# HGRN q, HGRN gate and the second value columns of w_in by seven half-size products

## The chip, the cores and the metric

The kernel runs on one core of one Trainium2 chip. The metric is device time in microseconds (us), lower is better; the kernel before was timed in three runs, median 2907.5 us (2903.78 to 2909.04). Besides these, one execution was profiled.

## The reference

One layer of a bidirectional encoder with two parallel groups of heads, for 1024 tokens of 2048 channels, in float32:

```python
u = rmsnorm(h, g_pre)
z = u @ w_in                                   # (1024, 2048) x (2048, 9216)
aq, ak, av, ag, hq, hf_f, hf_b, hv, hg = jnp.split(z, SPLIT_IDX, axis=-1)   # 1024 columns each
...                                            # dilated attention from aq, ak, av -> o_att
y_att = o_att * jax.nn.silu(ag)
qh = jax.nn.silu(heads(hq, HG_HEADS))          # 8 heads of 128
vh = heads(hv, HG_HEADS)
o_fw = hgrn2_direction(qh, vh, heads(hf_f, HG_HEADS), lb_f)
o_bw = jnp.flip(hgrn2_direction(jnp.flip(qh, 1), jnp.flip(vh, 1),
                                jnp.flip(heads(hf_b, HG_HEADS), 1), lb_b), 1)
y_hg = rmsnorm(o_fw + o_bw, g_hg).reshape(B, S, HG_W) * jax.nn.silu(hg)
h = h + rmsnorm(jnp.concatenate([y_att, y_hg], axis=-1) @ w_out, g_post)
h = h + rmsnorm(jax.nn.sigmoid(h @ w_pg) * (p @ w_pp), g_ple)
```

`hgrn2_direction` is a gated linear recurrence over the tokens, with f = lb + (1 - lb) * sigmoid(f_logit) as forget gate and 1 - f as key.

## The kernel before

**Products in three parts.** Each float32 matrix product is done as three products: a high part of the activations times the high part and times the low part of the weights, and a low bfloat16 part of the activations times a bfloat16 copy of the weights. The normalised activations u lie transposed in SBUF for the whole projection: `uh` (high, two tiles of 128 channels x 16 channel blocks x 512 tokens, one for each half of the tokens) and `ul` (low, the same shape). A *piece* of weights is 128x512 elements: `raw` is loaded on SP's queue, ScalarE copies it to `wh` (L82), GpSimd subtracts to get the low part `wl` (L83), VectorE casts it to `wb` (L84). Each of `raw`, `wh`, `wl`, `wb` has three buffers. GpSimd and ScalarE and VectorE are called POOL, ACT and DVE in the profile.

**Order of the stages.** First the eight token tiles are normalised and transposed (`prenorm`), with the first value group (columns 2048 to 2559) worked off in between, for tiles 0 and 1, for 2 and 3, and for 4 to 7 (its second half, four token tiles: 12 products of 512 columns for each piece). Then come three value groups `v_group(1)` to `v_group(3)` over all eight token tiles (24 products for each piece, 16 pieces); 2 and 3 are the value columns of the HGRN heads (7168 to 8191). They go through DRAM (`vD`). Then the eight HGRN heads, then the eight pairs of attention heads, then the output product and the gated embedding.

**A head of HGRN.** `hgrn` projects 128 columns at a time with `group` (16 blocks of channels in four pieces, 24 products each, into two PSUM banks of 512 tokens): the forward gate f0, the backward gate f1, q, and late in the head the output gate. `sink_f` takes f0 and f1 out of PSUM (sigmoid on ACT L240, scaling on DVE L241, into `F2`), `gate_evac` takes out q and the gate (x * sigmoid(x), L225 and L226). From f0 and f1 come X and O (L259 to L261, DVE) and their sum KD (L264, POOL); POOL also multiplies neighbouring gates for the next levels (`TB`, L334). The first small products use KD and q (`pl`). Seven levels of the recurrence follow, each some DVE operations (L281) and 32 small products on TensorE (L275, L300, L307). Then transposes (L351), the chunk states (L366 on TensorE, L370 and L372 on DVE), the output products `pout` (L385 to L389), the norm (L391, L392, `rstd2`) and `hon` (L398); `finish` transposes, multiplies by the gate and stores, and is issued after the f0 group of the next head.

**What sets the order.** The kernel is written stage by stage, but the framework's scheduler places the instructions on the engines; `piece` raises the priority of weights outside the value groups. Each engine, and each DMA queue, then works through its own list in order. `gb()` gives four PSUM banks to projections (two groups ahead), `wk()` four to everything else. The buffer `hq` is also that of the transposed keys `hk0` (tag "hq"), and `gt` has one buffer.

## Time and profile before

| | us |
|---|---|
| median of three runs | 2907.5 |
| profiled execution | 2911.69 |
| its span, from the first to the last instruction | 2909.9 |
| first value group with the norm, to | 142 |
| value groups 1, 2, 3, to | 228, 314, 401 |
| HGRN heads, about | 401 to 1314 |
| attention, about | 1314 to 2051 |
| output product and embedding | 2051 to 2910 |

| engine | busy us | share |
|---|---|---|
| TensorE | 2785.7 | 96% |
| VectorE (DVE) | 1508.4 | 52% |
| ScalarE (ACT) | 925.5 | 32% |
| GpSimd (POOL) | 1023.8 | 35% |

The profile is one execution. Matmuls are pipelined, so that the duration of one (about 390 ns) is longer than the time from one to the next, and a TensorE that waits a little between products still looks busy. A row of the view in order of time has start, duration, engine, line, operation, output<-inputs, shape and count, and in brackets the idle time ahead of it and what ended it. A row of a view by stretches has the busy time of each engine in the stretch, then the granted clock of TensorE, the share of the DMA engines and GB/s.

### The profile page before, as it was taken

The numbers are of one execution on the slowest core, as the hardware profiler recorded it, in microseconds if no ns is written. First come the engines' busy times: TensorE is split into PE (matmuls) and PEld (weight loads), VectorE is DVE, ScalarE is ACT, GpSimd is POOL, SyncE is SP. The second block draws the span as 40 slices with busy tenths as digits, with TensorE's granted clock in tenths as the row PEclk, the third lists the DMA queues.
The fourth block names the chain that finished last, engine by engine and source line by source line (L and its number), as shares of the span: only waits on it lengthen the run. The fifth ranks groups of instructions, "written<-read, shape, count | busy, mean of one in ns | idle before, by whom it ended". The sixth has DMA issues, their size and how long they took to land. (4 is left out here: it accounts for less than half of the span.)

```text
span 2909.9 us, 46582 instructions
## 1 busy us (share of the span) xinstructions
PE 2785.7 (96%) x18128; PEld 1885.7 (65%) x18384; DVE 1508.4 (52%) x2833; ACT 925.5 (32%) x1672; POOL 1023.8 (35%) x769
## 2 busy tenths in 40 slices
PE   6999999999999999999999999999999899999997
PEld 4666666676667676676666666666566566665664
DVE  8601116856346346356655555555755645555555
ACT  5311112222122112124434444443533223333323
POOL 2422223413313313322222222222244554666555
PEclk9999999999999999999999999999999999999998
DMA  6412221211111111121221222122344543433453
GB/s 226 121 55 80 77 86 39 66 52 39 57 52 44 52 52 45 51 65 55 78 70 45 73 76 71 47 74 71 113 122 133 159 142 97 131 113 109 146 155 106
DMA packets 251614, 250.54 MB, mean 86 GB/s; under 512 B 21633, under 2 KB 175233, under 8 KB 250241
## 3 DMA queue, kind: packets, MB, share of 16 engines
q1 hardware_dynamic: 242224, 238.62, 27.6%
q10 hardware_dynamic: 9168, 8.93, 0.9%
q8 instruction: 144, 2.36, 0.3%
q14 instruction: 78, 0.63, 0.1%
HBM read 205.54 MB, written 29.36 MB: 81 GB/s over the span
## 5 line engine op out<-in xcount | busy, mean ns | idle before, releaser
L83 POOL TENSOR_TENSOR wl<-raw,wh 128x512 fp32r<-128x512 f32 x568 | 764.7, 1350 | 1599.8 <-ACT wh L82 1507.1
L84 DVE CAST wb<-raw 128x512 bf16<-128x512 f32 x584 | 430.5, 740 | 785.2 <-PE gb L106 281.8
L82 ACT CAST wh<-raw 128x512 fp32r<-128x512 f32 x584 | 358.4, 617 | 1241.7 <-PE gb L101 414.7
L101 PE MATMUL gb<-uh,wh 128*128 128x512 f32 x1792 | 744.3, 415 | 0.0
L102 PE MATMUL gb<-uh,wl 128*128 128x512 f32 x1792 | 708.6, 395 | 0.0
L106 PE MATMUL gb<-ul,wb 128*128 128x512 bf16 x1632 | 405.7, 380 | 9.8 <-issue 1.8
L101 PEld LDWEIGHTS gb<-uh,wh 128*128 128x128 f32 x1792 | 337.1, 188 | 82.9 <-issue 1.2
L102 PEld LDWEIGHTS gb<-uh,wl 128*128 128x128 f32 x1792 | 337.1, 188 | 68.9 <-issue 1.0
L106 PEld LDWEIGHTS <-wb 128*128 128x128 bf16 x1792 | 158.4, 98 | 204.6 <-issue 54.3
L810 PE MATMUL gb<-wh,yh 128*128 128x512 f32 x512 | 231.2, 452 | 2.8 <-DVE Y L842 2.8
L810 PE MATMUL gb<-wh,th 128*128 128x512 f32 x480 | 215.8, 450 | 0.0
L811 PE MATMUL gb<-wl,yh 128*128 128x512 f32 x512 | 203.7, 398 | 4.7 <-POOL wl L83 4.7
L811 PE MATMUL gb<-wl,th 128*128 128x512 f32 x480 | 190.6, 397 | 5.4 <-POOL wl L83 5.4
L645 DVE CUSTOM_DVE_ANT_1 asm<-asc,amask 128x512 f32<-128x512 f32 x128 | 88.3, 690 | 119.9 <-PE asc L639 119.7
L814 PE MATMUL gb<-wb,yl 128*128 128x512 bf16 x479 | 133.7, 383 | 1.6
L814 PE MATMUL gb<-wb,tl 128*128 128x512 bf16 x452 | 126.2, 384 | 1.0
L650 ACT ACTIVATE asm<-asm,anm 128x512 f32<-128x512 f32 x128 | 92.5, 722 | 90.3 <-DVE anm L648 90.0
L810 PEld LDWEIGHTS gb<-wh,yh 128*128 128x128 f32 x512 | 97.6, 191 | 33.3 <-DVE Y L842 3.3
L737 PE MATMUL gb<-wh,uh 128*128 128x512 f32 x256 | 116.4, 461 | 1.4 <-ACT wh L82 1.3
L811 PEld LDWEIGHTS gb<-wl,yh 128*128 128x128 f32 x512 | 97.4, 190 | 24.3 <-POOL wl L83 5.9
L738 PE MATMUL gb<-wl,uh 128*128 128x512 f32 x256 | 102.4, 407 | 10.9 <-POOL wl L83 7.9
L634 PE MATMUL asc<-ak,aqt 128*32 128x256 bf16 x1536 | 109.7, 401 | 3.2 <-issue 2.4
(274 smaller groups left out, 3668.4 us busy)
## 6 DMA issues: line engine op xcount, KB each, us to landing
raw<-in_w_in_dram SPq DMA_DIRECT2D x320, 256.0 KB
raw<-in_w_out_dram SPq DMA_DIRECT2D x128, 256.0 KB
raw<-in_w_pg_dram SPq DMA_DIRECT2D x128, 256.0 KB
xt<-in_x_dram SPq DMA_DIRECT2D x8, 1024.0 KB
vD<-vo SPq DMA_DIRECT2D x32, 256.0 KB
raw<-yD SPq DMA_DIRECT2D x32, 256.0 KB
xr<-in_x_dram SPq DMA_DIRECT2D x32, 256.0 KB
ak<-ak SPq DMA_DIRECT2D x96, 64.0 KB
```

The source lines that it names most:

```text
L82: nc.scalar.copy(wh, raw)
L83: (sub or nc.gpsimd).tensor_tensor(wl, raw, f32(wh), op=ALU.subtract)
L84: nc.vector.tensor_copy(wb, raw)
L101: nc.tensor.matmul(pb[hf], wh[:, k], self.uh[hf][:, kt], start=(kt == 0), stop=False)
L102: nc.tensor.matmul(pb[hf], wl[:, k], self.uh[hf][:, kt], start=False, stop=False)
L106: mm = nc.tensor.matmul(pb[hf], wb[:, k], self.ul[hf][:, kt], start=False, stop=(kt == KT - 1))
L634: t = nc.tensor.matmul(sc[32 * r:32 * r + 32, :256], qb[:, sq, 32 * r:32 * r + 32], KS[s][:, h, r::4], start=(s == 0), stop=False, skip_gr ...
L737: nc.tensor.matmul(pb[t], hi, wh, start=(k == 0), stop=False)
L738: nc.tensor.matmul(pb[t], hi, wl, start=False, stop=False)
L810: nc.tensor.matmul(pb[t], a, pc[0], start=first, stop=False)
L811: nc.tensor.matmul(pb[t], a, pc[1], start=False, stop=False)
L814: nc.tensor.matmul(pb[t], lo[:, k, 128 * t:128 * t + 128], pc[2], start=False, stop=last)
```

## The change

q, the output gate and the second value columns (1024 columns of `w_in` each) are no longer computed by eight products of half the size (two halves of the tokens, of the channels and of the columns) but by seven, after Winograd's form of Strassen's scheme. It needs sums of blocks on both sides:

- **On the activations**, four sums S1 to S4 of blocks of u, the same for all three. `s_build` makes them, for each of the eight channel blocks of a half, with twelve additions and subtractions (nine on DVE, three on POOL) and four copies on ACT, and stores them to DRAM in high and low parts (`sD`). In the text it stands behind `v_group(1)`.
- **On the weights**, T1 to T4. `Block.weights` makes them for each piece: T2 loads three blocks and makes two subtractions and keeps the result in `TB`, T3 loads two and makes one, T1 and T4 load one and subtract `TB`, and three products take a block as it is.
- `Block.product` issues one of the seven: eight pieces of 128 channels, 12 products each into four PSUM banks. The products go in turn to two sets of four banks, two of them on top of what stands there. `Block.run` adds up the four blocks of the result with copies on ACT and additions on DVE.
- The value columns go to `vD` as before. q and the gate are multiplied by their sigmoid (ACT and POOL, `z_out`) and go to DRAM as `zD`, in the order of the heads, ahead of all heads; a head of HGRN loads its rows of them (two loads of 0.5 MB on SP's queue) where it had two groups of products.
- The constants of the heads are placed behind the second value group and the sums; the tiles of `prenorm` get a pool of their own, and `vo` a buffer name that is shared.

```diff
         self.group(w_in, base + 2048, sink_f(1))
         q = big.tile([128, S], F32, name="hq", tag="hq", bufs=1)
-        self.group(w_in, base, lambda hf, p: self.gate_evac(q[:, 512 * hf:512 * hf + 512], p))
+        nc.sync.dma_start(q, self.zD["hq"][h])
...
         gt = big.tile([128, S], F32, name="hgt", tag="gt", bufs=1)
-        self.group(w_in, base + 4096, lambda hf, p: self.gate_evac(gt[:, 512 * hf:512 * hf + 512], p))
+        nc.sync.dma_start(gt, self.zD["hg"][h])
...
+    def s_build(pool, kk):
...
+        (a11, l11), (a12, l12), (a21, l21), (a22, l22) = [
+            (f32(K.uh[r][:, kk + 8 * c]), K.ul[r][:, kk + 8 * c]) for r in range(2) for c in range(2)]
+        x0, x1, x2 = x("sx0"), x("sx1"), x("sx2")
+        add(x1, a21, l21, nc.gpsimd)
+        add(x2, a22, l22, nc.gpsimd)
+        add(x0, a11, l11)
+        add(x2, x1, x2)
+        s2 = x("sx3")
+        sub(s2, x2, x0)
+        sub(x1, x0, x1)
+        sub(x0, a12, s2)
+        add(x0, x0, l12)
+        for i, t in enumerate((x2, s2, x1, x0)):
+            h = pool.tile([128, 512], F32R, name="sxh", tag="sxh", bufs=3)
+            l = pool.tile([128, 512], BF16, name="sxl", tag="sxl", bufs=3)
+            nc.scalar.copy(h, t)
+            sub(l, t, f32(h), nc.gpsimd if i == 3 else V)
+            nc.sync.dma_start(sD[i][0][:, kk], f32(h))
+            nc.sync.dma_start(sD[i][1][:, kk], l)
...
+        def raw(self, kk, r, c, second=False):
+            if second:
+                t = ring_pool[0].tile([128, 512], F32, name="rb", tag="rb", bufs=4)
+            else:
+                t = K.wp.tile([128, 512], F32, name="raw", tag="raw", bufs=3)
...
+            elif name == "T2":
+                t = self.raw(kk, 0, 1)
+                sub(t, t, self.raw(kk, 0, 0, True))
+                d = self.TB[:, kk]
+                sub(d, self.raw(kk, 1, 1, True), t)
+                t = d
+            elif name == "T1":
+                t = self.raw(kk, 1, 1)
+                sub(t, t, self.TB[:, kk])
+            elif name == "T3":
+                t = self.raw(kk, 1, 1)
+                sub(t, t, self.raw(kk, 0, 1, True))
+            else:
+                t = self.raw(kk, 1, 0)
+                sub(t, t, self.TB[:, kk])
...
+            nc.scalar.copy(wh, t)
+            sub(wl, t, f32(wh), nc.gpsimd)
+            V.tensor_copy(wb, t)
...
+                for c in banks:
+                    mm(c, hi, wh, first and kk == 0, False)
+                    mm(c, hi, wl, False, False)
+                for c in banks:
+                    mm(c, lo, wb, False, kk == 7)
...
+        def run(self):
...
+                        nc.sync.dma_start(f32(h), sD[i][0][:, 4 * q:4 * q + 4])
+                        nc.sync.dma_start(l, sD[i][1][:, 4 * q:4 * q + 4])
...
+            self.product(0, orig(0, 0), "11", True)
+            c1 = self.copies(0, "tA")
...
+            self.product(1, orig(0, 1), "21", True)
+            for c in range(4):
+                add(c1[c], c1[c], self.pb[1][c])
+                self.out(0, 0, c, c1[c])
...
+            self.product(0, comb(1), "T2", False)
+            u = self.copies(0, "tB")
...
+            self.product(1, comb(0), "T1", True)
+            p5 = self.copies(1, "tA")
+            self.product(0, comb(2), "T3", False)
...
+            self.product(1, comb(3), "22", False)
...
+            self.product(0, orig(1, 1), "T4", False)
...
+    def z_out(name, pool):
+        def f(r, n, c, t):
+            sg = pool.tile([128, 512], F32, name="zsg", tag="zsg", bufs=2)
+            nc.scalar.activation(sg, t, AF.Sigmoid)
+            nc.gpsimd.tensor_tensor(t, t, sg, op=ALU.mult)
+            nc.sync.dma_start(zD[name][4 * n + c][:, 512 * r:512 * r + 512], t)
...
         v_group(0, (4, 5, 6, 7), p0)
+        v_group(1, tuple(range(8)), p0)
+        with tc.tile_pool(name="p0s", bufs=1) as p0s:
+            for kk in range(8):
+                s_build(p0s, kk)
         with tc.issue_after(late[0].ins), tc.issue_after(late[1].ins):
             K.hg_consts((lb_fwd, lb_bwd), g_hg)
-        for cg in range(1, 4):
-            v_group(cg, tuple(range(8)), p0)
+        with tc.tile_pool(name="p0r", bufs=1) as p0r:
+            ring_pool[0] = p0r
+            Block((7168, 7680), False, v_out(2), p0, False).run()
+            Block((8192, 8704), True, z_out("hg", p0), p0, True).run()
+            Block((4096, 4608), True, z_out("hq", p0), p0, False).run()
```

What stands in the built programs at the places in question (line numbers of each program's own source). First DVE, behind the last normalised tile (L151 writes the low part of u), where the second half of the first value group begins. Before, the casts of its pieces (L84) stand there with the small constants of the heads:

```order
L151 TENSOR_TENSOR ul_97<-xp,uh_95 128x4x128 x10
L84 CAST wb<-raw 128x512
L186 TENSOR_SCALAR hgi<-hgi 128x32
L422 TENSOR_SCALAR ab<-api 128x1
L422 TENSOR_SCALAR arho<-api 128x1
L187 TENSOR_TENSOR hgx<-hgi,hgj 128x32
L422 TENSOR_SCALAR atl<-ab 128x1
```

Now, at the same place (L753 and L756 are the additions and subtractions of `s_build`):

```order
L151 TENSOR_TENSOR ul_97<-xp,uh_95 128x4x128 x10
L84 CAST wb<-raw 128x512
L753 TENSOR_TENSOR sx_1837<-uh_94,ul_96 128x512
L753 TENSOR_TENSOR sx_1839<-sx_1838,sx_1839 128x512
L84 CAST wb<-raw 128x512
L756 TENSOR_TENSOR sx_1844<-sx_1839,sx_1837 128x512
L756 TENSOR_TENSOR sx_1838<-sx_1837,sx_1838 128x512
L756 TENSOR_TENSOR sxl<-sx_1839,sxh 128x512
L756 TENSOR_TENSOR sx_1837<-uh_94,sx_1844 128x512
L84 CAST wb<-raw 128x512
```

The scheduler has moved the sums ahead of the second value group: about four of them stand between two casts of the first one's second half. Of the 72 on DVE, 49 stand ahead of the cast for its last piece. On POOL, before, the subtractions L83 stand alone for the value groups:

```order
L83 TENSOR_TENSOR wl<-raw,wh 128x512 x85
L512 MEMSET apart_4066 128x512
L512 MEMSET apart_4067 128x512
L83 TENSOR_TENSOR wl<-raw,wh 128x512 x6
L334 TENSOR_TENSOR TB<-F_2954 128x1024
```

Now, from the start (19 pieces; POOL has every second piece of the first half of that group, and three of its second half):

```order
L83 TENSOR_TENSOR wl<-raw,wh 128x512 x19
L753 TENSOR_TENSOR sx_1838<-uh_95,ul_97 128x512
L753 TENSOR_TENSOR sx_1874<-uh_95,ul_97 128x512
L753 TENSOR_TENSOR sx_1839<-uh_95,ul_97 128x512
L753 TENSOR_TENSOR sx_1875<-uh_95,ul_97 128x512
L83 TENSOR_TENSOR wl<-raw,wh 128x512 x2
L753 TENSOR_TENSOR sx_1911<-uh_95,ul_97 128x512
L83 TENSOR_TENSOR wl<-raw,wh 128x512
L753 TENSOR_TENSOR sx_1910<-uh_95,ul_97 128x512
```

Of the 24 on POOL, 17 stand ahead of the subtraction for the last piece of that group. Then TensorE in the middle of the heads, where a head's first small products (`pl`, from KD and q) stand. Before, the 96 products of the q group come between the second gate group and these, and the gate group has begun (L101 and L102 are the high products of a group, L106 the low ones):

```order
L106 MATMUL gb<-ul_97,wb 128x512
L101 MATMUL gb<-uh_94,wh 128x512
L102 MATMUL gb<-uh_94,wl 128x512
L101 MATMUL gb<-uh_94,wh 128x512
L275 MATMUL pl<-hq,KD 32x32 x16
L102 MATMUL gb<-uh_94,wl 128x512
L101 MATMUL gb<-uh_94,wh 128x512
L275 MATMUL pl<-hq,KD 32x32 x16
```

Now the second gate group is the last ahead of them, with the 16 high products of the first piece of the next head (whose end is seen here) in between:

```order
L101 MATMUL gb<-uh_95,wh 128x512
L102 MATMUL gb<-uh_95,wl 128x512
L275 MATMUL pl<-hq,KD 32x32 x32
L275 MATMUL pl<-Q_9540,X 32x32 x32
L106 LDWEIGHTS wb
L106 MATMUL gb<-ul_96,wb 128x512
```

Every head from the third on has this order; in the second 56 products stand in that place. Further on, 51 products of the next head stand between the small products of the levels, 10 among the states and the first `pout`, 20 between `pout` and the transposes of `hon`, and 111 from there to the next head's `pl`, 192 in all.

94 lines of the change are left out of this document (88 added, 6 removed).

## The prediction

> **What bounds the kernel now.** First the page's table of engines, for the busiest engine; then the busy times by stage, because a mean over stages with different limits says little.
>
> ```profile
> PE 2785.7 (96%) x18128; PEld 1885.7 (65%) x18384; DVE 1508.4 (52%) x2833; ACT 925.5 (32%) x1672; POOL 1023.8 (35%) x769
> ...
> 98.00:142.00 44.00, 43.90 (x192) 29.10 (x196) 25.04 (x79) 12.40 (x22) 19.31 (x15) 1.00 0.38 92
> 228.00:314.00 86.00, 85.74 (x376) 58.79 (x382) 9.06 (x21) 11.79 (x20) 19.92 (x16) 1.00 0.25 74
> 314.00:401.00 87.00, 86.74 (x381) 59.26 (x387) 10.06 (x22) 12.77 (x22) 20.73 (x17) 1.00 0.24 73
> 401.00:1314.00 913.00, 882.32 (x7790) 634.00 (x7881) 482.28 (x943) 200.09 (x328) 269.37 (x207) 1.00 0.18 54
> ```
>
> The second to fifth rows are the second half of the first value group, the two value groups that the change replaces, and the HGRN heads; columns are PE, PEld, DVE, ACT, POOL busy, granted clock, DMA share, GB/s. TensorE is full in all four, at full clock. So a removed product is worth its issue interval, as long as something else keeps TensorE fed. The interval comes from the casts of a value group, which keep step with the products:
>
> ```profile
> 153.38 0.43 DVE L84 CAST wb<-raw 128x512 bf16<-128x512 f32 x1 [4.86 <-PE vb L741]
> ...
> 223.49 0.43 DVE L84 CAST wb<-raw 128x512 bf16<-128x512 f32 x1 [4.97 <-PE vb L741]
> ```
>
> Thirteen pieces lie between these casts: 5.393 us per piece of 24 products, 0.2247 us per product. What the second value group shows as idle, DVE at a tenth, looks like free room for the sums; the order of the changed program shows that they don't stand there.
>
> **The gain.** q, gate and the two value columns cost 2304 products (768 each); seven eighths is 2016. 288 x 0.2247 = **-64.7 us**. The products stay the same form, so neither the interval nor this term is in doubt; what follows eats into it.
>
> **The sums.** `s_build` adds 72 DVE and 24 POOL operations. In the changed order 49 of the DVE ones and 17 of the POOL ones stand ahead of the weights of the last piece of the first value group's second half, whose last 14 pieces (after two that are ready) still need their `wl` and `wb`. What DVE and POOL do to each other is the question:
>
> ```profile
> 2137.20 0.69 DVE L799 TENSOR_TENSOR yl<-raw,yh 128x512 bf16<-128x512 f32 x1 [1.09 <-ACT yh L798]
> 2137.82 1.53 DVE L84 CAST wb<-raw 128x512 bf16<-128x512 f32 x1
> ...
> 2137.77 1.29 POOL L83 TENSOR_TENSOR wl<-raw,wh 128x512 fp32r<-128x512 f32 x1 [1.94 <-ACT wh L82]
> ...
> 65.17 2.35 DVE L167 SCALAR_TENSOR_TENSOR xt<-xt,xr,gpre 128x2048 f32<-128x2048 f32 x1
> 67.44 1.49 DVE L84 CAST wb<-raw 128x512 bf16<-128x512 f32 x1
> 68.85 1.76 DVE L83 TENSOR_TENSOR wl<-raw,wh 128x512 fp32r<-128x512 f32 x1
> ...
> 65.75 4.32 POOL L83 TENSOR_TENSOR wl<-raw,wh 128x512 fp32r<-128x512 f32 x2 [5.09 <-ACT wh L82]
> ```
>
> The cast of 0.43 takes 1.53 and ends where POOL's operation has ended. Further up two POOL operations of 1.29 take 4.32, since the first can't begin before DVE's of 2.35 is through, and DVE's subtraction of 0.69 takes 1.76 behind the second. So the two engines take turns: casts and two-input operations of DVE never run beside a POOL operation, and their times add. Every operation of `s_build` has two inputs in SBUF. The Trainium skill, "SBUF — State Buffer", section "Who interferes with whom", says the same: a DVE instruction with two SBUF inputs and a GpSimd instruction that reads SBUF exclude each other for a whole instruction. The trace agrees (1.53 against 0.43); without that rule the two engines would overlap, and the build would cost 1 us by the lower bound below.
>
> Start to start, DVE's subtraction takes 0.62 (2137.20 to 2137.82). So 49 x 0.62 + 17 x 1.29 + 14 x (1.29 + 0.43) = 30.4 + 21.9 + 24.1 = 76.4 us of turns.
>
> ```profile
> 94.14 6.14 DVE L151 TENSOR_TENSOR ul<-xp,uh 128x512 bf16<-128x512 f32 x10 [0.57 <-ACT uh L150]
> ...
> 141.90 1.29 DVE L744 COPY vo<-vb 128x512 f32<-128x512 f32 x2 [0.87 <-PE vb L741]
> ```
>
> The sums can't begin before the last activations, at 100.3; the last weights come at 176.7 and their 12 products end at 179.4. Before, they ended at 141.9: **+37 us**. Bounds: if the engines overlapped, POOL alone with 31 x 1.29 = 40.0 ends at 143, +1; if each of DVE's operations waited as in the 1.76 and 1.49 rows, 49 x 1.76 + 14 x 1.49 = 107 us, +68. I take the sum of turns, which is how the rows add up. The rest of the sums (23 and 7) has all of the second value group, 86 us, and is free there. The 64 stores on SP's queue, among the raw loads, move 12.6 MB over more than 80 us, half the rate below.
>
> **The products with two subtractions.** T2 reads three weight blocks per piece where a piece now has 12 products, 2.70 us. The 228 to 314 row moves 74 GB/s at a share of 0.25, so about 296 GB/s at full load (an estimate). T2 loads 24 x 0.262 = 6.3 MB, and beside it go four stores (1.05 MB) and a half of the next sums (1.57 MB): 8.9 MB, 30.1 us, of which 7 blocks (6.2 us) fit the buffers ahead. That is 23.9 us where the last piece is wanted after 18.9: 5 us in each of three blocks, **+15**. Turns of POOL and DVE, 1.29 + 0.43 + 2 x 0.62 = 2.96 per piece, and in the second and third block four multiplications by the sigmoid (5.2) make 23.7 to 28.8 us, of which two ready pieces (5.9) are done before: 18 to 23 against the same 18.9. They lie under the same wait and are not added. Bounds: 0 if the buffers spread it; with nothing ahead 8.5, and T3 (7.3 MB, 24.8 us against 21.6) 3.2 more: 35. The other five products load and split less than 2.70 us per piece; the evacuations fall on the other four banks.
>
> **The heads.** Two of four projections leave each head, 43.1 of
>
> ```profile
> L264 POOL TENSOR_TENSOR KD<-X,O x8: 2392/3280/3282, 449.9 to 1208.8; 128x1024 f32<-128x1024 f32 x8
> ```
>
> (1208.8 - 449.9) / 7 = 108.4 us. That is counted in the gain. But the q group was also cover:
>
> ```profile
> 876.59 1.90 PE L106 MATMUL gb<-ul,wb 128*128 128x512 bf16 x8
> 878.14 0.58 PE L101 MATMUL gb<-uh,wh 128*128 128x512 f32 x1
> ...
> 900.70 0.46 PE L275 MATMUL pl<-hq,KD 128*32 128x32 f32 x32
> ...
> 879.16 0.55 DVE L241 TENSOR_SCALAR F<-F,omlb,lb 128x512 f32<-128x512 f32 x1
> ...
> 880.52 2.13 DVE L260 TENSOR_SCALAR O<-F 128x512 f32<-128x512 f32 x1
> ...
> 901.52 1.23 DVE L262 TENSOR_TENSOR Q<-hq,F 128x1024 f32<-128x1024 f32 x1
> ...
> 879.79 2.58 POOL L334 TENSOR_TENSOR TB<-F 128x1024 f32<-128x1024 f32 x1 [1.22 <-DVE F L241]
> 882.45 1.10 POOL L334 TENSOR_TENSOR TB<-TB 128x512 f32<-128x512 f32 x1
> 883.51 3.28 POOL L264 TENSOR_TENSOR KD<-X,O 128x1024 f32<-128x1024 f32 x1
> ```
>
> The second gate group of a head ends at 878.14. Sigmoid, scaling, two products TB and then KD on POOL end at 886.79, and all 8.65 us lay under the q group; the small products on KD came at 900.70. Now only 16 products of the next head (3.6 us) stand between. TensorE waits 5.05 us in seven heads (in the second head 56 products stand there): 35. At the end of a head:
>
> ```profile
> 942.38 0.39 PE L387 MATMUL pout<-hst,Q 128*128 128x128 f32 x2
> ...
> 946.65 1.29 DVE L398 TENSOR_TENSOR hon<-pout,hr 128x512 f32<-128x512 f32 x2
> ```
>
> the way from the last pout to the normalised tiles takes 5.6 us (to 947.94), under the next head's group; now 20 products, 4.5 us: about 1 us, eight times: 8. Between these ends DVE is the pace,
>
> ```profile
> 907.00:934.00 27.00, 23.64 (x452) 18.06 (x455) 26.40 (x56) 6.47 (x11) 4.75 (x3) 1.00 0.08 22
> ```
>
> (26.4 of 27 us from the second level to the last state), and its operations stay, so fewer products beside them save nothing there: they are what TensorE lacks later. **+43 us.**
>
> What is moved out of the heads costs nothing by itself:
>
> ```profile
> L82 ACT CAST wh<-raw 128x512 fp32r<-128x512 f32 x584 | 358.4, 617 | 1241.7 <-PE gb L101 414.7
> ...
> L225 ACT ACTIVATE sg<-gb 128x512 f32<-128x512 f32 x32 | 19.1, 597 | 10.9 <-PE gb L106 10.9
> ```
>
> the sigmoids (0.6 on ACT) come back in the blocks, where ACT has 0.62 per piece of 2.70 to do. The loads of q and gate (0.5 MB, two per head) go through SP's queue, q behind the wait for the transposed keys that share its buffer, with the raw loads of two later pieces behind it; 125 products (28 us) stand between its issue and its use, and three raw and three split buffers stand between. Without that cover a load from issue to use, as long as a piece, would show in each head.
>
> Bounds of the heads: 8 if KD is covered after all; 72 if DVE's Q product (1.23) pushes KD back and the clock below takes all it can.
>
> A waiting TensorE also slows down:
>
> ```profile
> 68.70 1.12 PE L738 MATMUL gb<-wl,uh 128*128 128x512 f32 x2 [2.13 <-POOL wl L83]
> ...
> 68.00:70.00 2.00, 1.30 (x4) 1.00 (x5) 2.00 (x2) 0.00 (x0) 2.00 (x2) 0.71 0.04 5
> 70.00:72.00 2.00, 2.00 (x8) 1.57 (x8) 2.00 (x5) 0.89 (x2) 0.07 (x1) 0.50 0.50 135
> 72.00:74.00 2.00, 2.00 (x9) 1.36 (x9) 1.71 (x6) 0.32 (x1) 0.00 (x0) 0.94 0.81 247
> ```
>
> After a wait of 2.1 us the granted clock is 0.5 for some 3.5 us, 1.75 us lost. A wait of 5 us in a head will do that; part of it falls on DVE's time: 1 us, seven times, **+7**. The Trainium skill, "TensorE: Matmul & The Clock Gate", part 1, wants an idle window of about 3.4 us for it; by that rule the heads' 5 us would do, by the row shorter waits too, and the sum is the same.
>
> **Sum.** -64.7 + 37 + 15 + 43 + 7 = +37 us. The profiled execution took 2911.7 (span 2909.9 and 1.8 around it), 4 above the median of 2907.5; I put the difference on the median: **2945 us**.
>
> **Rivals.**
> - *Heads stay fed* (not slower): the wait for KD at the head's start decides; its price is 42 of the 50 us. For it: KD's inputs X and O are ready at 882.6, and only the order on POOL puts TB first. Against: 3.6 us of cover for 8.65. Then 2903; above 1 us per head left of the 6, the sign is slower.
> - *Sums overlap*: the engines don't exclude each other for these operations, build +1: 2909. Against it are the rows above. Both together: 2866, faster.
> - *The transfers decide*: T2 and T3 at their upper bound (35) and the heads at 64: 2986. For it: 250 GB/s on average over a block (37.8 MB in 151 us) against 296; against it: the ring loads have long rows.
> - That the count isn't seven eighths is excluded: each block issues 7 x 96 products.
>
> **Chances.** Forecast 0.61; transfers 0.15; heads fed 0.10; sums overlap 0.07; both 0.07. A measurement tells about 0.2% (6 us) from no change. Faster: both, 0.04 of heads fed, 0.02 of overlap, 0.13. Same: 0.05 and 0.04, 0.09. Slower: the rest, 0.78. The range 2897 to 2992 leaves out both together, and the ends of the others.
>
> **What would show it.** The second half of the first value group should end near 179 us, TensorE waiting there for POOL's wl; the second group takes 86 us. Blocks should take 151.0 us of products each and some 5 more, waiting in T2. Heads should repeat every 71 to 72 us with one wait of 5 us ahead of the KD products, and a clock of 0.5 behind it. If the value group ends before 150, or heads repeat in 66, I am wrong.

## The result, and the profile after

The changed kernel takes 2980.5 us (median of four runs, 2974.4 to 2991.5) against 2906.1 (2903.8 to 2909.0): **slower by the factor 1.026**, 95% interval 1.0224 to 1.0295. The profiled execution took 2974.35 with a span of 2972.6, 62.7 more than the span before.

First the engines from the page of the changed kernel, then its busy times by stage (columns as in the table of before: PE, PEld, DVE, ACT, POOL, granted clock, DMA share, GB/s):

```profile
PE 2757.8 (93%) x17841; PEld 1847.2 (62%) x18096; DVE 1800.0 (61%) x3099; ACT 1001.2 (34%) x1810; POOL 1232.3 (41%) x897
...
98.00:142.00 44.00, 33.69 (x129) 20.48 (x130) 44.00 (x44) 13.07 (x23) 32.05 (x22) 0.92 0.55 159
142.00:180.00 38.00, 24.56 (x77) 14.96 (x79) 36.03 (x49) 11.65 (x22) 24.59 (x17) 0.82 0.53 171
180.00:262.00 82.00, 81.74 (x360) 56.22 (x365) 25.66 (x77) 16.14 (x28) 25.18 (x19) 1.00 0.51 176
262.00:746.00 484.00, 467.09 (x1981) 306.56 (x2018) 278.30 (x332) 143.07 (x241) 268.75 (x197) 0.99 0.67 225
746.00:1396.00 650.00, 563.44 (x6336) 412.33 (x6402) 459.88 (x856) 143.45 (x240) 214.68 (x151) 0.96 0.21 63
```

TensorE lost only 28 us of busy time where 64.7 us of products went, and it now stands idle in three stages: the end of the first value group and the start of the second (first two rows, DVE full or nearly, clock down to 0.82), the blocks (262 to 746) and the heads (746 to 1396). Only the third row, the rest of the second value group, is as full as before.

By stage, from the start of one stage's first product to that of the next:

| stage | before | after | without waits | lost |
|---|---|---|---|---|
| to the first product of value columns 2 | 228.5 | 261.8 | 228.5 | +33.3 |
| products by seven, three blocks (before: two value groups) | 172.9 | 483.8 | 453.0 | +30.8 |
| heads, up to the first scores of the attention | 929.0 | 650.5 | 583.9 | +66.6 |
| all behind | 1579.5 | 1576.5 | | -3.0 |

The third column counts the 2016 products of the blocks at 0.2247 us each and takes 8 x 192 products off the heads; together that is the forecast gain of 64.7. 33.3 + 30.8 + 66.6 - 3.0 - 64.7 = 63.0, the difference of the spans (62.7) but for rounding.

**The first value group and the start of the second**, from the waits of TensorE between 98 and 262 (what waited, for whom; us in total, times, longest), and then, in order of time, where the second group begins:

```profile
PE vb L738 <- POOL wl L83: 15.0, 8, 3.0
PE vb L737 <- DVE vo L744: 3.9, 1, 3.9
PE gb L738 <- POOL wl L83: 3.9, 1, 3.9
...
163.03 1.02 PE L741 MATMUL vb<-wb,ul 128*128 128x512 bf16 x4 [0.20 <-DVE wb L84]
163.70 0.58 PE L737 MATMUL gb<-wh,uh 128*128 128x512 f32 x1
...
176.26 0.76 PE L737 MATMUL vb<-wh,uh 128*128 128x512 f32 x1 [3.92 <-DVE vo L744]
```

18.9 us of waiting are for POOL's low part, as forecast, and 3.9 for DVE's copy of the finished group out of PSUM, which stands behind the sums. With the lower clock of the first two rows above (44 x 0.08 + 38 x 0.18, about 10 us) that makes up the 33.3. The place is only in part the forecast one: the first group's second half ends at 163.7 (before 142.2), 21.5 us late, and the first piece of the second group takes from 163.7 to 180.9, 12 us longer than the 5.4 before.

**The blocks.** A piece without a wait isn't 12 x 0.2247 = 2.696, as the first two pieces show:

```profile
261.82 0.58 PE L841 MATMUL gb<-wh,uh 128*128 128x512 f32 x1
...
264.54 0.59 PE L841 MATMUL gb<-wh,uh 128*128 128x512 f32 x1
```

2.72 us; where the activations come from DRAM it is 2.71 in the first block and 2.75 in the other two. A product of eight pieces takes 21.7 to 22.0 without a wait, 459 us in all: 6 of the 30.8. The other 25 us lie in these products (start to start):

| product | 11 | 21 | T2 | T1 | T3 | 22 | T4 |
|---|---|---|---|---|---|---|---|
| first block | 21.8 | 21.8 | 21.7 | 21.7 | 22.2 | 25.0 | 23.8 |
| second (gate) | 21.8 | 21.8 | 24.6 | 22.0 | 22.0 | 22.0 | 27.3 |
| third (q) | 21.8 | 21.8 | 26.4 | 22.0 | 22.0 | 22.5 | 27.8 |

T2 and T4 of the second block, first TensorE's wait in each, then DVE and POOL in T2 and SP's queue in T4; the last three rows are the stretches of T2 in the first block and of T4 in the second and third (columns as above):

```profile
477.17 0.50 PE L839 MATMUL vb<-rh,wl 128*128 128x512 f32 x1 [2.05 <-POOL wl L756]
565.78 0.80 PE L839 MATMUL vb<-uh,wl 128*128 128x512 f32 x1 [2.81 <-POOL wl L756]
...
470.85 3.46 DVE L756 TENSOR_TENSOR raw<-raw,rb 128x512 f32<-128x512 f32 x2
...
472.04 3.41 POOL L916 TENSOR_TENSOR tA<-tA,zsg 128x512 f32<-128x512 f32 x2
...
475.41 4.83 POOL L756 TENSOR_TENSOR wl<-TB,wh 128x512 fp32r<-128x512 f32 x3
...
567.17 0.32 SPq L917 DMA_DIRECT2D zhg<-tB  x1
567.59 1.34 SPq L797 DMA_DIRECT2D raw<-in_w_in_dram  x3
...
305.00:327.00 22.00, 21.95 (x98) 14.73 (x98) 17.71 (x23) 4.72 (x8) 11.16 (x8) 1.00 0.86 288
554.00:581.00 27.00, 23.57 (x94) 15.18 (x95) 17.79 (x21) 8.30 (x14) 17.85 (x13) 0.94 0.60 199
717.00:745.00 28.00, 24.84 (x99) 15.39 (x100) 18.55 (x20) 7.93 (x13) 18.31 (x13) 0.94 0.39 123
```

At 470.85 two subtractions of DVE (0.69 each when alone) take 3.46 and stand between POOL's multiplications by the sigmoid (L916), two in 3.41; the low parts (L756) come behind both. In T4 the last store of a multiplied result goes at 567.17, and the next raw loads stand behind it on SP's queue: they go at 567.59. So two candidates remain for T4, turns of the engines or SP's queue, and the forecast's transfers for T2; the experiments part them. The last three rows already speak against the number of bytes: T2 of the first block moves 288 GB/s and loses nothing, while T4, which loses most, moves 123 to 199. The waits in the blocks are 15 us in all; of the rest of the 25, some 5 are the lower clock behind three of them (564 to 570, 640 to 644 and 736 to 740, by 1 minus the granted clock). Not every wait is followed by it: after the 2.05 us at 477 the clock stays at 1.00.

**The heads.** The group of KD in the changed kernel, and TensorE's waits from 746 to 1396:

```profile
L264 POOL TENSOR_TENSOR KD<-X,O x8: 2337/3316/3318, 794.1 to 1311.9; 128x1024 f32<-128x1024 f32 x8
```

```profile
PE pl L275 <- POOL KD L264: 49.0, 8, 15.8
PE po L405 <- DVE hon L398: 10.5, 8, 1.3
PE pu L366 <- DVE hk L352: 7.2, 8, 1.1
PE pa L275 <- DVE Q L281: 6.9, 8, 1.0
```

Seven of the eight waits for KD are about 4.75 us (forecast 5.05), one, in the second head, is 15.8. From KD to KD it is 93.2, 62.3, 73.0, 72.7, 72.4, 72.2, 72.1 us; before it was 114.7, 101.9, 108.3, 108.6, 108.3, 108.6, 108.3. A head without q and gate would take 108.4 - 43.1 = 65.3, so the last five lose 7.2 each (6.8 to 7.7), and the first two 25 together; some 6 lie behind the eighth KD. A steady head, for TensorE, DVE and POOL, and the clock behind the wait:

```profile
1098.54 1.08 PE L275 MATMUL pl<-hq,KD 128*32 128x32 f32 x64 [4.75 <-POOL KD L264]
...
1094.23 2.06 DVE L262 TENSOR_TENSOR Q<-hq,F 128x1024 f32<-128x1024 f32 x1
1096.21 3.25 DVE L281 TENSOR_TENSOR X<-X,F 128x512 f32<-128x512 f32 x1
...
1091.45 2.58 POOL L334 TENSOR_TENSOR TB<-F 128x1024 f32<-128x1024 f32 x1 [1.22 <-DVE F L241]
1094.11 1.10 POOL L334 TENSOR_TENSOR TB<-TB 128x512 f32<-128x512 f32 x1
1095.17 3.32 POOL L264 TENSOR_TENSOR KD<-X,O 128x1024 f32<-128x1024 f32 x1
...
1096.00:1100.00 4.00, 1.46 (x108) 1.46 (x112) 4.00 (x3) 0.00 (x0) 3.95 (x2) 0.74 0.01 4
```

Q (1.23 before) and the first X of the levels now fall beside TB and KD, and take 2.06 and 3.25. In the second head, DVE works off other things at this place:

```profile
889.65 0.58 PE L275 MATMUL pl<-hq,KD 128*32 128x32 f32 x25 [15.84 <-POOL KD L264]
...
853.53 0.68 DVE L496 SCALAR_TENSOR_TENSOR aang<-anh,aang 128x512 f32<-128x512 f32 x1
...
874.35 0.68 DVE L496 SCALAR_TENSOR_TENSOR aang<-anh,aang 128x512 f32<-128x512 f32 x1
874.95 0.54 DVE L241 TENSOR_SCALAR F<-F,omlb,lb 128x512 f32<-128x512 f32 x1
```

L496 is one of the lines that make the constants of the attention (masks and angles, L439 to L509, 60 operations from 839 to 893); the gates' own L241 stands among them.

### The profile page after: what moved, and what is told of

It is laid out like the page before. It is cut to its first block, busy times and chain, and to the rows that moved or that the text cites. A ratio compares the mean times of both kernels' runs of the same rounds, so it can differ in the third digit from the quotient of the medians.

```text
span 2972.6 us, 47521 instructions
## 1 busy us (share of the span) xinstructions
PE 2757.8 (93%) x17841; PEld 1847.2 (62%) x18096; DVE 1800.0 (61%) x3099; ACT 1001.2 (34%) x1810; POOL 1232.3 (41%) x897
## 5 line engine op out<-in xcount | busy, mean ns | idle before, releaser
L83 POOL TENSOR_TENSOR wl<-raw,wh 128x512 fp32r<-128x512 f32 x472 | 655.2, 1393 | 1196.6 <-ACT wh L82 1129.4
L84 DVE CAST wb<-raw 128x512 bf16<-128x512 f32 x488 | 380.1, 782 | 469.0 <-PE gb L996 211.0
L82 ACT CAST wh<-raw 128x512 fp32r<-128x512 f32 x488 | 299.0, 616 | 767.1 <-PE gb L101 239.9
L101 PE MATMUL gb<-uh,wh 128*128 128x512 f32 x1280 | 536.9, 419 | 0.2 <-ACT vo L902 0.2
L102 PE MATMUL gb<-uh,wl 128*128 128x512 f32 x1280 | 507.4, 396 | 0.0
L106 PE MATMUL gb<-ul,wb 128*128 128x512 bf16 x1145 | 295.1, 387 | 10.7 <-issue 3.8
L101 PEld LDWEIGHTS gb<-uh,wh 128*128 128x128 f32 x1280 | 241.5, 189 | 61.7 <-issue 2.0
L756 POOL TENSOR_TENSOR wl<-raw,wh 128x512 fp32r<-128x512 f32 x144 | 194.6, 1358 | 188.8 <-ACT wh L825 166.1
L102 PEld LDWEIGHTS gb<-uh,wl 128*128 128x128 f32 x1280 | 241.3, 189 | 47.9 <-issue 1.0
L106 PEld LDWEIGHTS <-wb 128*128 128x128 bf16 x1280 | 113.9, 99 | 146.2 <-issue 47.7
L827 DVE CAST wb<-raw 128x512 bf16<-128x512 f32 x144 | 122.5, 859 | 98.8 <-DMA raw<-in_w_in_dram 26.9
L825 ACT CAST wh<-raw 128x512 fp32r<-128x512 f32 x144 | 89.0, 618 | 276.1 <-DVE raw L756 112.2
```

The lines of the kernel that those rows point to most:

```text
L82: nc.scalar.copy(wh, raw)
L83: (sub or nc.gpsimd).tensor_tensor(wl, raw, f32(wh), op=ALU.subtract)
L84: nc.vector.tensor_copy(wb, raw)
L101: nc.tensor.matmul(pb[hf], wh[:, k], self.uh[hf][:, kt], start=(kt == 0), stop=False)
L102: nc.tensor.matmul(pb[hf], wl[:, k], self.uh[hf][:, kt], start=False, stop=False)
L106: mm = nc.tensor.matmul(pb[hf], wb[:, k], self.ul[hf][:, kt], start=False, stop=(kt == KT - 1))
```

## The experiments

Each kernel is the changed one with the edit shown, unless another is named. "Before" is the kernel before on the same chip, 2908.7 to 2910.3 us in the four sets of runs; the ratio is to that, with its interval. "Block" times are from start to start, as above.

### Holding the sums back: sums_held

```diff
             for kk in range(8):
-                s_build(p0s, kk)
+                a, b, c = marks[2 * kk]
+                with tc.issue_after(a.ins), tc.issue_after(b.ins), tc.issue_after(c.ins):
+                    s_build(p0s, kk)
```

(`marks` holds the copy, subtraction and cast of each piece of the second value group; `issue_after` places the build behind them on their engines.)

> Only the place of the sums differs from the changed kernel: each of the eight parts of the build is held on DVE, POOL and ACT behind every second piece of the second value group (24 products a piece), with the same operations on the same engines. Theory (DVE's and POOL's operations take turns, and the place decides): the second half of the first value group ends near 142 us again, not near 179; in the second value group the turns are 24 x 1.29 + 72 x 0.62 + 16 x 1.72 = 103 us against 86 of products, of which about 94 stand ahead of the last weights, so that group grows by 8 to 13; the first block begins 20 to 26 us earlier than 261.8, and the time is about 2955 to 2960. Rival 1 (the sums don't exclude the splits; they only stood in the way of casts): the first block begins near 228, all 33.6 us back, about 2947. Rival 2 (the stores of the sums or the loads set the end, not the engines): no gain, the wait moves into the second value group, about 2980.

Measured: 2958.6 us, ratio 1.0176 [1.0161, 1.0192]. Busy times by stage of this kernel:

```profile
98.00:142.00 44.00, 43.89 (x193) 29.06 (x196) 25.35 (x80) 12.18 (x21) 21.94 (x17) 1.00 0.37 92
142.00:233.00 91.00, 87.33 (x380) 59.21 (x386) 79.83 (x92) 29.16 (x50) 54.29 (x39) 1.00 0.58 192
```

The first value group is as before, and the wait there is gone. The second value group takes 5 us longer than 86, less than the 8 to 13 expected, and the first block begins 28.7 us earlier, more than the 20 to 26 expected. But the first product of that block takes 30.4 us in place of 21.8. Its raw loads stand on SP's queue behind the loads of the sums and the stores of the value group's results, while the DMA engines are full:

```profile
243.00:248.00 5.00, 3.13 (x14) 1.82 (x12) 0.47 (x1) 0.00 (x0) 0.00 (x0) 1.00 1.02 410
```

28.7 - 8.6 = 20 us are back, near the 22 of the medians. Part of what stays lost lies behind the group, in the block's transfers, and not in the turns where the theory had it. The profiled execution was the slowest of its four runs; its blocks took 500.0 us, which includes the 8.6.

### The same on DVE alone: sums_held_dve

On top of sums_held:

```diff
-        add(x1, a21, l21, nc.gpsimd)
-        add(x2, a22, l22, nc.gpsimd)
+        add(x1, a21, l21)
+        add(x2, a22, l22)
...
-            sub(l, t, f32(h), nc.gpsimd if i == 3 else V)
+            sub(l, t, f32(h))
...
-                                 sub=V if len(toks) == 2 and k % 2 else None)
+                                 sub=V if cg == 1 or len(toks) == 2 and k % 2 else None)
```

> As the kernel with the held sums, but all twelve operations of each part of the build on DVE, and the low parts of the second value group's pieces on DVE too, so that POOL has nothing in that stretch. Theory (turns): DVE alone needs 96 x 0.62 + 16 x (0.69 + 0.43) = 77 us of the 86, POOL never holds it, so the second value group takes 86 to 88 us and the first block begins at 228 to 231 us against 261.8: 31 to 34 us back, about 2948. Rival (DVE's queue is what was too long, whoever shares its port): DVE has more to do here than in the held kernel (77 against 59 us), so it gains no more than that one, or less. Rival (stores or loads): no gain, about 2980.

Measured: 2949.3 us, ratio 1.0142 [1.0126, 1.0157]; the first block begins at 227.5, 34.3 us earlier. The second value group:

```profile
142.00:228.00 86.00, 85.74 (x378) 59.08 (x384) 71.31 (x125) 28.55 (x50) 3.82 (x3) 1.00 0.70 235
```

DVE has 125 operations in these 86 us against 92 in the held kernel's 91, and yet is busy for less (71.3 against 79.8 us), since POOL has almost nothing to do here and hardly any of them stands still for it. TensorE doesn't wait. This shows the turns: moving POOL's work onto the fuller engine made that engine's stretch shorter. The Trainium skill, "SBUF — State Buffer", section "Who interferes with whom", has DVE's instructions with two SBUF inputs and GpSimd's reads exclude each other; this pair of runs agrees.

### Low parts of the blocks on DVE: blocks_low_dve

```diff
             nc.scalar.copy(wh, t)
-            sub(wl, t, f32(wh), nc.gpsimd)
+            sub(wl, t, f32(wh))
             V.tensor_copy(wb, t)
```

> In the three blocks by seven the low part of each piece of weights is subtracted on DVE (0.69 us) in place of POOL (1.29); loads, stores and their order in the text stay. In the changed kernel the blocks take 483.8 us, 25 of them beyond the steady 2.72 to 2.75 us per piece: T2 2.7 and 4.6, T4 2.0, 5.4 and 6.0, the sixth product 3.3 and 0.5. Theory (turns of DVE and POOL): T2 and T4 lose nearly all of it, since DVE needs at most 2.36 us of a piece's 2.72 and POOL has only the multiplications by the sigmoid: blocks 463 to 468 us, time about 2960 to 2964. Rival 1 (transfers, as the prediction had it): the waits of T2 stay at 2.7 and 4.6, and the whole gain is under 6 us. Rival 2 (SP's queue: loads stand behind stores that wait for the multiplications): T4 keeps 4 to 6 us in the second and third block, the gain is 5 to 10.

Measured: 2958.7 us, ratio 1.0174 [1.0157, 1.0191]. The blocks take 463.9 us. TensorE's waits in them, in the changed kernel (first rows) and here:

```profile
PE vb L839 <- POOL wl L756: 5.7, 4, 2.8
PE gb L839 <- POOL wl L756: 4.2, 4, 2.0
PE vb L841 <- POOL wl L756: 2.0, 2, 1.1
PE gb L841 <- POOL wl L756: 1.3, 2, 1.0
```

```profile
PE vb L839 <- DVE wl L756: 2.3, 3, 1.5
```

All that is left are T2 and T4 of the second block (23.8 and 24.2) and 0.9 in the third. The same bytes move through the same queue, so transfers weren't what T2 waited for. The edit takes away both POOL's own queue (low parts behind multiplications) and the turns; that DVE's subtractions of 0.69 took 3.46 for two in the changed kernel shows the turns at work, but the runs don't part the two shares.

### Stores behind the loads: blocks_stores_later

```diff
+                if kk == 7:
+                    with tc.issue_after(self.load.ins):
+                        while later:
+                            nc.sync.dma_start(*later.pop(0))
...
-            nc.sync.dma_start(zD[name][4 * n + c][:, 512 * r:512 * r + 512], t)
+            later.append((zD[name][4 * n + c][:, 512 * r:512 * r + 512], t))
```

(The same for `vD`; the last quarter of each block is stored at once. `self.load` is the last load of weights.)

> In the three blocks the stores of the first three quarters of the results are put on SP's queue behind the eighth raw load of the product that runs meanwhile, in place of at its start; nothing else. Theory for T4 and for the sixth product of the first block (loads wait on SP's queue behind stores whose data come late): their 13 + 3 us go, T2's waits (2.7 and 4.6) go at most by half: blocks 466 to 470 us, time 2962 to 2968. Rival 1 (turns of DVE and POOL alone): no stage changes by more than 1 us, about 2980. Rival 2 (transfers): the same bytes move in the same time, the waits change place, under 4 us.

Measured: 2972.2 us, ratio 1.0214 [1.0199, 1.023]. The blocks take 479.1 us; T4 is 26.3 and 26.9 in the second and third block, T2 25.3 and 24.8. Only the first block loses its waits in T4 (22.1) and half of those in 22 (23.0). So the theory of SP's queue is refuted for the second and third block, where most of the time is. For the first block, whose results aren't multiplied, it is supported by one profile: both times are below those of all six profiles in which these blocks are unedited (24.0 to 25.0 for product 22, 22.9 to 29.1 for T4).

### Cover for KD: heads_cover

```diff
+        if h < 7:
+            self.ahead = self.group_parts(w_in, base + 1152, lambda hf, p: self.sink0(hf, p))
+            for _ in range(4):
+                next(self.ahead)
         pt = self.wk("pl", (128, 2, 8, 32))
```

(The next head goes on with `self.ahead` where it began its first gate group.)

> In the first seven heads two pieces (48 products, 10.8 us) of the next head's first gate group stand ahead of the small products on KD, where 16 stood (56 in the second head); no operation is added or left out. From the end of the second gate group's products (1090.4) to the end of KD (1098.49) it is 8.1 us. Theory (the q group was the cover of the way to KD): the waits for KD, 49 us in all, go; a head takes 66 to 68 us in place of 74.0, the heads and what follows them begin 40 to 50 us earlier, the time is 2930 to 2940. Rival (the chain of DVE's operations sets the period, and TensorE only waits elsewhere: 48 products fewer beside the levels, DVE busy 52 of 74 us): the period stays at 71 us or more, the waits appear at pl from Q, pa and po, the gain is under 20 us.

Measured: 2946.1 us, ratio 1.0133 [1.0114, 1.0151]. The heads take 610.5 us in place of 650.5, 40.0 less. TensorE's two longest waits there:

```profile
PE pl L278 <- DVE Q L288: 15.3, 15, 1.3
PE pl L278 <- POOL KD L267: 14.8, 2, 10.1
```

The wait for KD is gone in six heads; it stays in the eighth (4.7, no next head) and in the second (10.1). From the second interval on it is 62.1 and then 66.2 to 66.5 from KD to KD, against 65.3 with no wait at all: DVE's chain doesn't set the period. The time is above the 2930 to 2940 expected. In the profiled execution that is the blocks, not edited here, which took 495.0 us, 11 more than in the changed kernel's first profile (see the last run).

### KD on DVE: heads_kd_dve

```diff
+        V.tensor_tensor(KD, X, O, op=ALU.add)
         V.tensor_tensor(Q2[:, 0], q, F2[:, 1], op=ALU.mult)
         V.tensor_tensor(Q2[:, 1], q, F2[:, 0], op=ALU.mult)
-        nc.gpsimd.tensor_tensor(KD, X, O, op=ALU.add)
```

> KD is added on DVE (two inputs of 128x1024, 1.3 us by the multiplication Q on the same size in the kernel before) ahead of Q, in place of POOL (3.3 us) behind the two products TB; 21 products of the next head stand ahead of the small products on KD, where 16 stood. Theory (the way to KD is what the head waits for): KD ends 2 to 3 us earlier, 1.1 us more of cover, so 3 to 4 us of the 4.75 go in each of seven heads, and Q and the first level follow one KD later: a head takes 70 to 71.5 us, gain 18 to 28 us, time 2953 to 2963. Rival 1 (DVE and POOL take turns here too: the addition on DVE waits for both TB, 3.7 us): KD ends at most 1 us earlier and the levels begin later, gain under 10 us. Rival 2 (the chain of DVE's operations sets the period): DVE has 1.3 us more in each head, 0 or slower by up to 10 us.

Measured: 2961.2 us, ratio 1.0182 [1.0164, 1.0201]; the heads take 629.5 us, 21 less, and 69.7 to 70.3 from KD to KD from the third on. The same place in a steady head of this kernel:

```profile
1090.27 0.72 PE L275 MATMUL pl<-hq,KD 128*32 128x32 f32 x62 [3.04 <-issue]
...
1086.56 2.06 DVE L263 TENSOR_TENSOR Q<-hq,F 128x1024 f32<-128x1024 f32 x1
1088.54 1.63 DVE L262 TENSOR_TENSOR KD<-X,O 128x1024 f32<-128x1024 f32 x1
```

The wait is 3.04 in place of 4.75. The gain is inside the theory's 18 to 28, though the scheduler put one Q ahead of KD, whose 2.06 us stand in the way that is left.

### One part alone: value_only

```diff
-        nc.sync.dma_start(q, self.zD["hq"][h])
+        self.group(w_in, base, lambda hf, p: self.gate_evac(q[:, 512 * hf:512 * hf + 512], p))
...
-            Block((8192, 8704), True, z_out("hg", p0), p0, True).run()
-            Block((4096, 4608), True, z_out("hq", p0), p0, False).run()
```

(The gate likewise.)

> Only the second value columns by seven products; q and the output gate are again groups of the heads, as in the kernel before. Theory (the parts add up as the stages show): the sums cost 33.6 us in the first value group, the block takes 158 us where two value groups took 173, the heads are as in the kernel before (929 us): +34 - 15 = +19 us, time 2925 to 2929; then the other two blocks and the heads bring the rest, 54 us. Rival (the sums would cost as much anywhere, and the heads lose also from what stands ahead of them): heads longer by 5 us or more, time above 2933. Rival (a block behaves otherwise where the heads follow it): the block's last two products lose 5 us or more against the changed kernel.

Measured: 2921.3 us, ratio 1.005 [1.0033, 1.0067]. This is 4 below the 2925 to 2929 expected. In the profiled execution (2927.1, the slowest of four) the block takes 155.6, the heads 929.4 us: the heads lose nothing by what stands ahead of them, only by what they no longer hold.

### The three edits together: all_three

The edits of sums_held_dve, blocks_low_dve and heads_cover in one kernel.

> The sums on DVE behind the second value group's pieces, the blocks' low parts on DVE, and 48 products of the next head ahead of KD. If the three losses lie in different stages and the theories hold: 2980.5 - 31 - 22 - 40 = 2887, between 2877 and 2900, faster than the kernel before (2908). Seven eighths of the products would give 2908 - 65 = 2843; what is left then is 168 x 0.03 to 0.05 us for pieces of half the size (6 to 7), waits of T2 and T4 (4 to 6) and heads of 66 to 68 us in place of 65.3. Rival (DVE sets the period of the heads): 2905 to 2925.

Measured: 2883.9 us (2881.6 to 2888.7), ratio **0.992** [0.9902, 0.9937]: faster than both kernels, by 0.8% than the kernel before. By stage:

```profile
142.00:229.00 87.00, 86.74 (x382) 59.68 (x389) 73.92 (x128) 29.85 (x53) 0.00 (x0) 1.00 0.70 234
229.00:695.00 466.00, 460.66 (x1980) 304.51 (x2016) 292.30 (x498) 142.77 (x241) 44.05 (x30) 1.00 0.72 240
695.00:1306.00 611.00, 555.49 (x6343) 407.27 (x6404) 464.06 (x856) 141.65 (x239) 224.12 (x152) 0.99 0.23 68
```

The losses are now 0.5 in the first stage (229.0), 13.4 in the blocks (466.4 against 453.0) and 27.1 in the heads (611.0 against 583.9); 14 of the latter are the first two intervals (84.1 and 62.4 against 66.3).

### Where the attention's constants can go: consts_split, consts_last

Both are all_three with one edit more. consts_split issues the constants in three parts, behind the first, second and third head (a generator with two `yield`); consts_last issues them in one piece behind the eighth:

```diff
-            if h == 0:
+            if h == 7:
                 with tc.issue_after(late[0].ins), tc.issue_after(late[1].ins):
                     K.att_consts(positions)
```

> As the kernel with all three edits, but the constants of the attention (masks and angles, some 50 operations of DVE that stand in one piece between the gates and X, O of the second head) are issued in three parts, behind the first, second and third head; 48 products of the next head stand ahead of KD in the second head too, where 67 stood. Theory (the wait of 10 us for KD in the second head is these constants ahead of X and O on DVE): it goes, each part finds room in its head while the next gates are computed, the heads take 8 to 10 us less, time 2873 to 2877. Rival (DVE has no such room: each part makes its own head wait): under 3 us, with a wait of 3 us or more for KD in the second, third and fourth head.

> As the kernel with all three edits, but the constants of the attention are issued behind the eighth head, in one piece, in place of behind the first. In the kernel with all three edits the first two head to head times are 84.1 and 62.4 us where the others are 66.2 to 66.5: 14 us beyond; split over three heads they cost 66.7 + 76.0 + 74.0 + 62.9, the same 14. Here 245 products of projections (55 us) stand ahead of the first scores of the attention, where 163 stood. Theory (some 30 us of DVE that must come in one head cost what that head's room can't hold; the first pair of the attention has products enough that don't need DVE): all seven head to head times 66 to 67 us, the first scores at most 4 us later after the last head than now, 8 to 14 us less: time 2870 to 2877. Rival (the scores wait for the constants just as KD did): the 14 us come back between the last head and the first scores or in the first pair, time 2880 to 2888.

Measured: 2884.1, ratio 0.9912 [0.9898, 0.9926], no gain; and 2890.6, ratio 0.9937 [0.9925, 0.9949], 7 us slower than all_three. Both theories fell. Split, the intervals are 66.7, 76.0, 74.0, 62.9: the same 14 us, spread. Behind the last head all intervals are 66.0 to 66.5, which shows that the constants are what the second head waited for; but the heads' 14.5 us come back ahead of the attention, whose first scores begin at 1321.3 in place of 1306.4. In shortened heads these operations have no free place. In the kernel before they had one: there the first two intervals sum to 216.6, twice 108.3.

### Two pieces at a time: consts_split_pairs

```diff
+                held.append((lo, wb))
...
-                for c in banks:
-                    mm(c, lo, wb, False, kk == 7)
+                if kk % 2:
+                    for i, (lo, wb) in enumerate(held):
+                        for c in banks:
+                            mm(c, lo, wb, False, kk == 7 and i == 1)
+                    held = []
```

(On top of consts_split, with four buffers of `wb` in place of three.)

> As the kernel with the split constants, and in the three blocks the low products of two pieces are issued together: 16 high products, 8 low ones, as in the value groups, in place of 8 and 4. Theory (a change between float32 and bfloat16 products costs a fixed time, 24 products in 5.393 us against 12 in 2.72 to 2.75: 0.06 to 0.08 us per change): two pieces take 5.39 to 5.40 us in place of 5.45 to 5.50, the products that don't wait take 21.6 us in place of 21.8 and 22.0, the blocks 5 to 7 us less. Rival (a piece of half the size costs by its loading or banks, not by the change): 21.8 and 22.0 stay. In both cases the splits are held longer (two bfloat16 copies at a time), so T2 and T4 can wait up to 5 us more.

Measured: 2892.7 us, ratio 0.9936 [0.9922, 0.9949]; 8.6 above consts_split, with intervals that just overlap. The start of three pairs of pieces in the first block:

```profile
224.80 0.58 PE L857 MATMUL gb<-wh,uh 128*128 128x512 f32 x1
...
230.19 0.58 PE L857 MATMUL gb<-wh,uh 128*128 128x512 f32 x1
...
235.59 0.58 PE L857 MATMUL gb<-wh,uh 128*128 128x512 f32 x1
```

5.39 to 5.40 for two pieces, as in a value group, in place of 5.45: in the three products of each block that work on u itself (11, 21, T4) the new order saves the 0.06 us, as the theory of a price for each change has it. In the four on the sums it saves little or nothing: they take 5.42 for two pieces in the first block with either order, and 5.47 to 5.48 in place of 5.50 in the others. So a fixed price for each change isn't shown; what decides between the two kinds stays open. The little gain goes into longer waits (single pairs of 7.55 and 10.13 us in T2 and T4 of the second block), and the blocks take 465.9 us against 465.7. The two profiled spans agree (2886.2 and 2886.4), but the one execution was the fastest of its five and the other the slowest; why the median is 8.6 higher stays open.

### The changed kernel again: changed_again

> The changed kernel once more, beside the others. The blocks took 483.8 us in its first profile and 487.5 to 495.0 in three kernels whose blocks are the same. If that is a difference from execution to execution, this one takes some other value between 480 and 495 and the sum of its other stages stays within 3 us; if it comes from the built order, it takes 483 to 485 again. Time 2974 to 2985 in either case.

Measured: 2985.9 us, ratio 1.0259 [1.0242, 1.0277]. The same program took 491.4 us in the blocks, and the sum of the other stages was 3.4 us above the first profile (3 were expected; the median is 1 us above the expected range). So the blocks of the changed kernel vary by 8 us and more from execution to execution; with the low parts on DVE, profiles of four kernels gave 463.9 to 466.6. The gain of that edit is therefore 20 us by the first profile and 27 by this one.

## Why the prediction was right in sign and low by 35 us

The forecast was +37 on the median, measured were +74 (2980.5 - 2906.1); the first profiled execution, the fastest of four, shows 63 of them. Of the 26 us between 37 and 63, 17 lie in the heads, 10 in the waits of the blocks and 6 in the length of a piece; the sums (-4) and the stages behind the heads (-3) go the other way. The other 11 are differences from execution to execution, to which the blocks may add most: 487 to 500 us in five further profiles of the same blocks, where this one has 483.8. By its own terms:

- **Products, -64.7.** The count is right. "Neither the interval nor this term is in doubt" is wrong by 6 us: a piece of 12 products takes 2.71 to 2.75 us and not 2.696. In the products on u the excess goes when the bfloat16 products of two pieces stand together; in the products on the sums the cause is open.
- **Sums, +37: +33.3.** Right in sign, in the engine (POOL's low part) and nearly in size, but the size is luck in part. The turns were put too long: the sums stood ahead of the last piece's weights as counted, but its low part was ready at 160.9, 60.6 us after the 100.3 and not 76.4. Four of POOL's sums had begun earlier (97.4 to 102.6); why the turns otherwise took less than the rows add up to isn't shown. So the first group ended at 163.7 and not near 179. And the second group, forecast at 86 us, took 98, for its first piece met the same turns. Some 10 of the 33 are the lower clock, which the forecast had in the heads alone. Held behind later pieces the sums cost less, on DVE alone nothing, so it was the turns with POOL and not the amount of work. One reading is to be set right: 1.53 against 0.43 is a cast, with one input; for two inputs the row is 1.76 against 0.69.
- **T2, +15 by transfers: 25, and not by transfers.** This step failed twice. T2 lost 0, 2.7 and 4.6 us, by the turns of DVE and POOL, which the forecast had worked out (18 to 23 us against 18.9) and then put under the transfers' wait. And the other products were taken to "split less than 2.70 us per piece": in T4 that sum leaves out that the results of the product before are added up and multiplied by the sigmoid in the same 22 us. In the second and third block T4's pieces and these results need up to 8 x (0.62 + 0.43 + 1.29) + 4 x 0.62 + 4 x 1.29 = 26.4 us of turns, the sum that the forecast made for T2 alone; less two ready pieces (4.7) it is 21.7 where the last piece is wanted after 18.9. TensorE waited 3.4 and 3.3 us there, and with the clock behind these waits (0.50 from 566 to 568 and from 737 to 739) T4 lost 13 us in the three blocks. blocks_low_dve takes nearly all of it away with the same loads; the queue of SP counted in the first block only, as far as one profile shows.
- **Heads, +43, and +7 by the clock: +66.6.** For a steady head the forecast was 50 / 7 = 7.1 us and 71 to 72 from KD to KD; measured were 7.2 and 72.1 to 73.0, with the wait where it was put (4.75 for 5.05), 1.3 at the head's end where about 1 was put, and the rest near the 1 us that was put for the clock. heads_cover gives 40 of it back, and its period of 66.2 to 66.5 shows that DVE's pace in the levels costs only about 1 us a head. What failed is the second head, counted as covered because 56 products stand there: TensorE waited 15.8 us in it, and its two intervals lost 25. The list of what DVE does at this place was read for a steady head and not for the one that also makes the attention's constants. The cover that the change takes out had hidden those too.
- **The rival "transfers decide", 2986,** came nearest in number and by the wrong mechanism. With the loads unchanged, the low parts on DVE took nearly all the waits away; the loads of the first block stand in a queue behind stores, which is another thing than too many bytes. Bytes did decide in one product, but in sums_held: the DMA engines are full there.
- **"Heads stay fed"** and **"sums overlap"** are refuted by the waits for KD and by the first value group.

Left of the 65 us, after the three edits, are 25 (ratio 0.992). The rest goes to the longer pieces (6), waits in T2 and T4 (7), the constants (14), and some 13 in the heads, of which 1 us in each steady one and 4.7 for the eighth's KD show in the rows above.

## What to carry to other kernels

Fewer products pay only where the removed ones weren't the cover of another engine's chain: before taking a group out, list what runs beneath it in every repetition, the odd one too, and put other work of TensorE in its place. Count the time of two engines that exclude each other as one sum per stretch, with the evacuation of the product before in it, and take it as an upper estimate (76 us by the rows were 61 here); if the sum passes TensorE's time, give the work to the faster of the two, even if that one is the busier. A scheduler that finds an engine idle early will move preparatory work in front of something urgent, so hold it back by an explicit order.

## What the runs showed of the hardware that was not expected

- The order of float32 and bfloat16 products can count: two pieces of 12 products on u take 5.39 us with their bfloat16 products together and 5.45 with them apart. Products whose activations are loaded during the block take 5.42 to 5.50, in the first block the same 5.42 in either order; no run shows why.
- Moving GpSimd's operations of one stretch onto VectorE lowered VectorE's busy time from 79.8 to 71.3 us, though it had 125 operations in place of 92: busy time includes the time that it stands still in a turn (two subtractions of 0.69 us took 3.46).
- One program's blocks took 483.8 and 491.4 us in two executions, with two engines taking turns close to TensorE's pace; without the turns profiles of four kernels agree within 2.7 us.
- After a wait of TensorE of 2.81 us the granted clock was 0.50 for the next two us, after one of 2.05 us it stayed at 1.00 (both in the second block).
